# Projection of a hybrid decoder trunk: another order of memory rows, norms and key turns, five low weight halves per part on VectorE, a pause for memory keys, and a pair at the head of the second part

## The chip, the cores and the metric

The kernel runs on one core of a Trainium2 chip. The metric is the device time of one execution in microseconds (us). Engines are named as the profile names them: PE is TensorE (PEld its weight loads), ACT is ScalarE, DVE is VectorE, POOL is GpSimd, and SP is the sync engine, which issues most DMAs.

## What is computed

One mixer layer with four head groups, for a prompt of 2048 rows and for a sample group of 8 x 4 rows. Cut to what matters here:

```
h = rms_norm(x, pre_g)
z = h @ w_in                       # 1024 -> 11 x 512: ca cb cg pu pg q k v sg mq mg
mk, mv = split(rms_norm(mem_prompt, mem_g) @ w_mem_kv)
y_c = conv branch(ca, cb)          # depthwise, width 31, LayerNorm, pointwise
y_p = pool branch(pu)
y_s = stick-breaking attention(q, k, v)    # the sample group reads a paged cache of 8192 tokens
y_m = softmax attention(mq, mk, mv)        # 256 memory tokens; the sample group has its own keys
mix = [y_c*silu(cg), y_p*silu(pg), y_s*silu(sg), y_m*silu(mg)]
out = x + rms_norm(mix @ w_out, post_g); y = rms_norm(out, final_g)
```

## The kernel before

The first 1491 us of the profiled span are the projection `x @ w_in`, and everything that the change touches lies in them. It runs in two parts of 1024 prompt rows; part 0 also carries the 32 sample rows. Before any product the normalised rows of x are transposed on PE, 128 rows and 512 features at a time, and split into a high half (`xhi`, copied by ACT) and a low half (`xlo`, the difference, on DVE): `split_rows`, L211. A weight block of 1024 x 128 is loaded (`load_w`, tile `wr`, two buffers), and `split_w` (L229) makes `whi` on ACT (L232) and `wlo` on POOL (L233), two buffers each. `mm3` (L236) then multiplies a tile of up to 512 columns with 24 products: whi with xhi, whi with xlo, wlo with xhi.

PE's order is the order of the Python code (`manual_schedule` for PE). For the other engines a list scheduler orders the instructions by its own estimate of when each is ready, so a later traced instruction may be queued first; `tc.issue_after(ins)` puts the instructions of a block behind `ins` on its engine. Each engine runs its queue in order.

The order of the projection is set by these pieces:

- `GROUPS` (L762): the list of groups of weight blocks. Most groups hold one block; a pair holds two, whose column tiles alternate. The pairs are (q0, q1), (mq, sg) for c = 0, 1, 2, (mq3, pg3) and (cg3, sg3). The column tiles (`COLS`) are 384, 384 and 288 wide in part 0, 512 and 512 in part 1. `z_groups` (L789) runs them and calls `fill_w` to split the next weights as soon as a block is done.
- `Tasks`: a list of generators, each advanced by one step at every half of a column tile (12 products). `x_first` (L281) and `x_stream` (L322) bring the x rows of part 0 and part 1, `mem_norm` (L379) the two blocks of memory rows, `sample_keys` (L431) turns the sample group's memory keys (8 batches; a load into tile `mkb`, eight transposes on PE, copies into `mkbT` on ACT, a store to `mkTd`), `conv_dw` (L605) runs the taps of the convolution on DVE (tile `cacc`, L617), `mem_attend` (L494) is the memory attention of one column tile of mq (tiles `ms`, `pr`, `pT`, `pL`, `my`), and `natural` writes k and v out row by row.
- A z tile can only start when its columns of x are split: `X["done", part]`. The rows of part 1 overwrite those of part 0, so `x_stream` also waits for `X["free"]`.
- The sample group's attention over the cache (`sample_setup` L841, `sample_stages` L928) runs beside it, paced by the products issued: gathers of keys (`kt`) and values (`vt`) by POOL, `turn` (L954), which transposes keys on DVE (L959) into the single tile `T` and then issues the next gather, `scores` on PE (L972, tile `sSA`), scans on DVE (L989) and `values` on PE (L1011, tile `sO`).

Tiles of tag `k4` share four buffers: the loaded rows of `x_stream` (`xtp`), the sample keys (`mkb`, `mkbT`), the split q, k and mq tiles (`hl`, `mh`), and `pT`, `pL` of the memory attention. A buffer is free for the next tile when its last reader is done; for a stored tile that is when the store has landed. PSUM tiles of tag `tp` (three banks) hold all transposes and small products; `x_first` has five buffers for its rows.

In `x_first` two norms are ahead of the transposes: row block i is split, then i + 5 is loaded and i + 2 normalised. Six half blocks are done before the first product. `mem_norm` starts when 768 columns are split; it loads and normalises both blocks in its first step, pauses for two steps and then splits half a block at each step. Behind the projection the attention over the prompt (from L1282) and the output products follow.

Of the kernel before, what the change touches and what calls it, by code (L numbers as in the profile page):

```python
# [57 lines left out]
X0 = 6  # L58
SEND = 0.97
XA = 3  # L60
KT = 2
WR = 2

# [23 lines left out]
def kernel(  # L87
# [141 lines left out]
    def split_w(raw, nm):  # L229
        lo = wp.tile([P, ND, P], F32R, tag="wlo", name=f"wlo{nm}", bufs=2)  # L230
        hi = wp.tile([P, ND, P], F32R, tag="whi", name=f"whi{nm}", bufs=2)
        act.copy(hi, raw)  # L232
        pool.tensor_tensor(out=lo, in0=raw, in1=hi.bitcast(F32), op=ALU.subtract)  # L233
        return hi, lo

    def mm3(ps, whi, wlo, xhi, xlo, c0, c1):  # L236
# [44 lines left out]
    def x_first(tile_):  # L281

        todo = [(xp[P * t : P * (t + 1), :], P, P * t, f"p0_{t}") for t in range(8)] + [(xs, NS, PART, "s")]
        xts = {}

        def load(n):
            if n < len(todo):
                xts[n] = tile_(f"xt{todo[n][3]}")
                sp.dma_start(xts[n][: todo[n][1]], todo[n][0])

        def norm(n):
            if n < len(todo):
                norm_rows(xts[n], todo[n][1], gpre)

        def split_next():
            it = next(iter(raw))
            with tc.issue_after(table[-1].ins):
                wsplit[it] = split_w(raw.pop(it), "%d%s%d" % it)

        load(0)  # L300
        gpre = big("gpre0")[:, :D]
        sp.dma_start(gpre, pre_g[0].partition_broadcast(P))
        load(1)
        next_raw()
        load(2)
        next_raw()
        load(3)
        load(4)
        norm(0)
        norm(1)  # L310
        for i, (_, rows, col, nm) in enumerate(todo):
            for hf in range(2):
                split_rows(xts[i], rows, xhi, xlo, col, hf, nm)
                if hf:
                    X["done", 0] = col + rows
                    if i < 2:
                        split_next()
                    load(i + 5)
                    norm(i + 2)
                yield  # L320

    def x_stream(part, ahead, tile_):  # L322

        todo = [(xp[PART * part + P * t : PART * part + P * (t + 1), :], P, P * t, f"p{part}_{t}") for t in range(8)]
        ready = []
        gpre = None
        loaded = []

        def norm():
            n, xt = loaded.pop(0)  # L330
            ready.append(norm_rows(xt, todo[n][1], gpre, rs1[:, n : n + 1]))

        for i, (src, rows, col, nm) in enumerate(todo):
            while len(ready) + len(loaded) < min(len(todo), i + ahead):
                n = len(ready) + len(loaded)
                xt = tile_(f"xt{todo[n][3]}")
                sp.dma_start(xt[: todo[n][1]], todo[n][0])
                if gpre is None:
                    gpre = big(f"gpre{part}")[:, :D]
                    sp.dma_start(gpre, pre_g[0].partition_broadcast(P))  # L340
                loaded.append((n, xt))
            if i == 0:
                yield
                yield
                norm()
            if loaded:
                norm()
            while X["free"] < col + rows:
                yield
            for hf in range(2):  # L350
                split_rows(ready[i], rows, xhi, xlo, col, hf, nm)
                if hf:
                    X["done", part] = col + rows
                yield
# [24 lines left out]
    def mem_norm(mp, M):  # L379
        mg_bc = mp.tile([P, D], F32, name="mg_bc", bufs=1)  # L380
        sp.dma_start(mg_bc, mem_g[0].partition_broadcast(P))
        M["hi"] = mp.tile([P, ND, NMEM], F32R, name="mhi", bufs=1)
        M["lo"] = mp.tile([P, ND, NMEM], F32R, name="mlo", bufs=1)
        rows = []
        for t in range(2):
            xt = mp.tile([P, D], F32, tag="xt", name=f"xtm{t}", bufs=XB)
            sp.dma_start(xt, mem_prompt[0, P * t : P * (t + 1), :])
            rows.append(norm_rows(xt, P, mg_bc))
        yield
        yield  # L390
        for t in range(2):
            for hf in range(2):
                split_rows(rows[t], P, M["hi"], M["lo"], P * t, hf, f"m{t}")
                yield
# [36 lines left out]
    def sample_keys():  # L431

        for b in range(NB):
            k_ = k4(f"mkb{b}", [P, 2, 512], F32)
            sp.dma_start(k_, cmk[b].rearrange("(t p) c -> p t c", p=P))
            for _ in range(4):
                yield
            kT = k4(f"mkbT{b}", [P, 4, NMEM], F32)
            for t in range(2):
                pt = tp_tile(f"smt{b}_{t}")  # L440
                for h in range(4):
                    pe.transpose(pt[:, P * h : P * (h + 1)], k_[:, t, P * h : P * (h + 1)], ident)
                act.copy(kT[:, :, P * t : P * (t + 1)], pt.rearrange("p (h n) -> p h n", h=4))
                yield
            wq.dma_start(mkTd[b], kT)
# [48 lines left out]
    def mem_attend(h, part, c0, np_, hl, gate, kv):  # L494
# [43 lines left out]
        dve.tensor_tensor(out=mo[:, :np_], in0=yps[:, :np_], in1=gate[:, c0 : c0 + np_], op=ALU.mult)  # L538
        a = PART * part + c0
        wq.dma_start(mix_rows(12 + h, a, np_), by_tile(mo[:, :np_]))  # L540

    def mem_transpose(t2, nj, pr, pT, pL, nm):
        ps = tp_tile(f"mpt{nm}_{t2}")
# [106 lines left out]
        for r0, r1, dst in rows:  # L650
            wq.dma_start(dst, o[r0:r1])

    state = {}

    def z_open(part, kind, c):

# [23 lines left out]
    def z_evac(part, kind, c, ti, c0, c1, ps, s):  # L680
# [61 lines left out]
        elif kind == "mq":  # L742
# [4 lines left out]
                                     op0=ALU.mult, op1=ALU.subtract)  # L747
            if N > np_:
                dve.tensor_copy(mqs[:, c, :], ps[:, np_:N])
            tasks.add(mem_attend(c, part, c0, np_, hl, state["g"], s["kv"]))  # L750

    def z_close(part, kind, c, s):
# [4 lines left out]
        elif kind == "pu":  # L757
# [2 lines left out]

    MAIN = ("ca", "cb", "pu", "cg", "pg", "mg")
    GROUPS = {0: [[("q", 0), ("q", 1)]] + [[(k, c)] for k in ("q", "k", "v") for c in range(2 if k == "q" else 0, 4)],  # L762
              1: [[(k, c)] for k in ("k", "v", "q") for c in range(4)]}
    for part in range(2):
        for c in range(3):
            GROUPS[part] += [[(k, c)] for k in MAIN] + [[("mq", c), ("sg", c)]]
        GROUPS[part] += ([] if part == 0 else [[("ca", 3)], [("cb", 3)]]) + [[("pu", 3)], [("mg", 3)], [("mq", 3), ("pg", 3)]]
        GROUPS[part] += ([[("ca", 3)], [("cb", 3)]] if part == 0 else []) + [[("cg", 3), ("sg", 3)]]
    SEQ_W = [(p_,) + it for p_ in range(2) for g in GROUPS[p_] for it in g]
    for i, at in ((0, 3), (1, 4), (2, 5), (3, 7), (4, 8), (5, 9), (6, 11), (7, 12)):  # L770
        SEQ_W.insert(at, (0, "mem", i))
# [69 lines left out]
    def sample_setup(sm, S):  # L841
# [35 lines left out]
        bp = tp_tile("bps")  # L877
        pe.matmul(bp[:, 0:1], lhsT=e8, rhs=bcol, start=True, stop=True)
        dve.tensor_copy(b1, bp[:, 0:1])
        dve.tensor_scalar(out=nb1, in0=b1, scalar1=-1.0, scalar2=None, op0=ALU.mult)  # L880
        S["b1"], S["nb1"] = b1, nb1

        rep = sm.tile([P, 4, 4, 32], F32, tag="vt", name="rep", bufs=VB)
# [44 lines left out]
    def sample_stages(sm, sps, S):  # L928
# [25 lines left out]
        def turn(n, ml):  # L954
            if n < N:
                T = sm.tile([P, 4, 16, 32], F32, tag="T", name=f"T{n}_{ml}", bufs=TB)
                kt = kts.pop((n, ml))
                for hh in range(2):
                    dve.transpose(T[:, 2 * hh : 2 * hh + 2].rearrange("p s j t -> p (s j t)"),  # L959
                                  kt[:, 2 * hh : 2 * hh + 2].rearrange("p s j d -> p (s j d)"))  # L960
                Ts[n, ml] = T
                load_k(n + 1, ml)

# [60 lines left out]
        load_v(0)  # L1024
        for _ in range(Y0):
            yield
        turn(0, 0)
        for n in range(N):
            yield
            scores(n, 0)  # L1030
# [1064 lines left out]
```

## Time and profile before

| | us |
|---|---|
| median of 3 runs | 2420.67 (2415.16 to 2429.53) |
| the profiled execution | 2418.47 |
| its span | 2416.7 |
| PE busy in the span | 2285.6 (95%) |
| DVE, POOL, ACT busy | 1718.3, 1306.8, 1117.5 |

How to read it: a row of a timeline gives the start, the duration, the engine, the line of the kernel, the operation, what it writes and reads with shapes, and in brackets how long the engine had stood idle before it and what ended that. A row of the waits gives the instruction that waited, what released it, the total in us, how often, and the longest. A row of the windows gives the stretch, its length, the busy us of PE, PEld, DVE, ACT and POOL with instruction counts, the granted clock of TensorE (1.00 is full), the share of the DMA engines and GB/s.

### The profile page before, as it was taken

The page shows a single profiled execution, that of the slowest core. Times are in us where ns is not written, and L with a number is a line of the kernel's source. Part 1 is how long each engine was busy: PE and PEld are TensorE (multiplying, and loading weights), DVE is VectorE, ACT ScalarE, POOL GpSimd, SP SyncE. Part 2 cuts the span into 40 slices and gives each one's busy share as a digit, 9 for nine tenths or more (in the row PEclk, how much of TensorE's full clock was granted, in tenths as well). Part 3 has the DMA queues.
Part 4 walks back from the last instruction along what each step waited for, and adds up shares of the span by engine and source line. Part 5 has one row for each costly group of instructions (what it writes and reads, how often), then busy time and mean ns, then how long its engine had stood idle before and what let it go on. Part 6 is the DMA issues. An engine that isn't in the chain of part 4 may idle for free. (4 is left out here: it accounts for less than half of the span.)

```text
span 2416.7 us, 42137 instructions
## 1 busy us (share of the span) xinstructions
PE 2285.6 (95%) x15962; PEld 1774.5 (73%) x15962; DVE 1718.3 (71%) x2410; ACT 1117.5 (46%) x1939; POOL 1306.8 (54%) x1333
## 2 busy tenths in 40 slices
PE   7999999999999999999999998899999998989897
PEld 6998978898888777777777776455555556768775
DVE  5333774959757664587877777879798846687998
ACT  5322343242442322124242434788989954443554
POOL 2554544556574555655556564667877755453430
PEclk9999999999999999999999999999999999999998
DMA  5789988887778899987887767834333227887764
GB/s 179 223 260 298 348 290 287 284 272 263 263 254 292 277 344 325 323 287 262 275 270 269 262 218 179 239 79 117 89 88 79 64 64 242 266 272 254 245 234 170
DMA packets 340437, 562.14 MB, mean 233 GB/s; under 512 B 28481, under 2 KB 212929, under 8 KB 323834
## 3 DMA queue, kind: packets, MB, share of 16 engines
q1 hardware_dynamic: 284858, 290.72, 39.2%
q0 software_dynamic: 55376, 268.72, 31.3%
q8 instruction: 126, 2.06, 0.3%
q14 instruction: 77, 0.63, 0.1%
HBM read 469.28 MB, written 90.68 MB: 232 GB/s over the span
## 5 line engine op out<-in xcount | busy, mean ns | idle before, releaser
L959 DVE STREAM_TRANSPOSE T<-kt 128x1024 f32<-128x1024 f32 x256 | 308.9, 1226 | 183.4 <-PE sSA L972 177.2
L926 POOL DMA_INDIRECT vt<-in_cache_v_dram,idv x256 | 251.6, 983 | 242.1 <-PE sO L1011 181.5
L617 DVE SCALAR_TENSOR_TENSOR cacc<-U,par,cacc 128x512 f32<-128x512 f32 x480 | 360.2, 750 | 11.8
L1311 POOL TENSOR_TENSOR be<-be,E 128x512 f32<-128x512 f32 (+2 forms) x320 | 303.8, 957 | 118.4 <-DVE E L1302 52.4
L1302 DVE TENSOR_TENSOR_SCAN E<-gam,cr,ZM 128x513 f32<-128x513 f32 x192 | 232.8, 1262 | 15.1 <-ACT gam L1287 14.2
L926 POOL DMA_INDIRECT kt<-in_cache_k_dram,idk x128 | 126.2, 986 | 201.9 <-DVE T L959 146.8
L1322 PEld LDWEIGHTS AT<-ident,be 128*128 128x128 f32 x1088 | 117.7, 142 | 127.6 <-ACT at L1328 45.4
L1287 ACT ACTIVATE gam<-S,nbias_bc 128x1024 f32<-128x1024 f32 (+1 forms) x160 | 172.6, 1079 | 50.8 <-ACT be L1289 18.9
L1915 PE MATMUL acc<-wohi,mh 128*128 128x512 f32 (+1 forms) x480 | 193.3, 403 | 0.6 <-ACT mh L1669 0.6
L1915 PE MATMUL acc<-wolo,mh 128*128 128x512 f32 (+1 forms) x480 | 189.6, 395 | 0.0
L1915 PE MATMUL acc<-wohi,ml 128*128 128x512 f32 x448 | 178.1, 398 | 11.6 <-DVE ml L1680 11.6
L1282 PE MATMUL S<-kT,Q 128*128 128x512 f32 (+1 forms) x640 | 177.9, 401 | 6.8 <-DMA Q<-qd 2.7
L1289 ACT ACTIVATE be<-S,bias_bc 128x1024 f32<-128x1024 f32 (+1 forms) x160 | 171.6, 1073 | 0.0
L1322 PE MATMUL AT<-ident,be 128*128 128x128 f32 x1088 | 158.1, 284 | 14.1 <-ACT at L1328 4.2
L1338 PE MATMUL av<-at,V 128*64 128x512 f32 (+3 forms) x640 | 153.0, 557 | 1.7 <-DVE sbo L1343 1.7
L972 PE MATMUL sSA<-T,W 128*32 128x128 f32 x4096 | 139.2, 277 | 6.4 <-DVE T L959 5.6
L972 PEld LDWEIGHTS sSA<-T,W 128*32 128x32 f32 x4096 | 104.7, 110 | 43.6 <-issue 35.3
L1680 DVE TENSOR_TENSOR ml<-mr,mh 128x512 fp32r<-128x512 f32 x108 | 98.1, 914 | 38.4 <-ACT mh L1669 38.2
L1282 PEld LDWEIGHTS S<-kT,Q 128*128 128x128 f32 x640 | 107.1, 195 | 23.0 <-ACT be L1289 3.5
L1011 PE MATMUL sO<-vt,saT 128*32 128x512 f32 x1024 | 122.4, 592 | 0.0
L1299 DVE TENSOR_TENSOR_SCAN E<-gam,ZM 128x128 f32<-128x128 f32 (+3 forms) x128 | 96.4, 802 | 30.1 <-ACT gam L1287 25.2
L1328 ACT COPY at<-AT 128x512 f32<-128x512 f32 x192 | 108.9, 655 | 14.4 <-PE AT L1322 14.4
(571 smaller groups left out, 6043.7 us busy)
## 6 DMA issues: line engine op xcount, KB each, us to landing
Q<-qd SPq DMA_DIRECT2D x64, 256.0 KB
mr<-mixd SPq DMA_DIRECT2D x32, 512.0 KB
mr<-mixd SPq DMA_DIRECT2D x48, 256.0 KB
wor<-in_w_out_dram SPq DMA_DIRECT2D x20, 512.0 KB
xtp<-in_x_prompt_dram SPq DMA_DIRECT2D x16, 512.0 KB
kT<-kd SPq DMA_DIRECT2D x64, 128.0 KB
wor<-in_w_out_dram SPq DMA_DIRECT2D x32, 256.0 KB
msd<-mr SPq DMA_DIRECT2D x32, 256.0 KB
```

What stands on the lines that cost most here:

```text
L617: dve.scalar_tensor_tensor(out=ps, in0=U[:, a + k : a + k + H], scalar=wd[:, k : k + 1], in1=ps, op0=ALU.mult, op1=ALU.add)
L926: pool.indirect_dma_start(out=dst, out_offset=None, in_=rows, in_offset=bass.IndirectOffsetOnAxis(ap=idx, axis=0))
L959: dve.transpose(T[:, 2 * hh : 2 * hh + 2].rearrange("p s j t -> p (s j t)"), kt[:, 2 * hh : 2 * hh + 2].rearrange("p s j d -> p (s j d)"))
L972: pe.matmul(sSs[n][32 * g : 32 * g + 32, P * ml : P * (ml + 1)], lhsT=W[:, jj, :], rhs=T[:, :, jj, :], start=i == 0, stop=i == 3, tile_pos ...
L1282: pe.matmul(S[:, j, :w], lhsT=Q[hh][:, x, P * (q2 + j) : P * (q2 + j + 1)], rhs=KT[hp, hh, kc][:, :w], start=x == 0, stop=x == 1)
L1287: act.activation(out=ga[:, :, 512 - w : 512], in_=S[:, :, :w], func=AF.Sigmoid, bias=nbias_bc[:, h : h + 1], scale=-1.0)
L1289: act.activation(out=be[:, :, :w], in_=S[:, :, :w], func=AF.Sigmoid, bias=bias_bc[:, h : h + 1])
L1302: dve.tensor_tensor_scan(out=E[:, j][:, ::-1], data0=ga[:, j][:, ::-1], data1=ZM[:, 0:1].to_broadcast([P, 513]), initial=carry[hh, q2][:, ...
L1311: pool.tensor_tensor(out=be[:, j, :m], in0=be[:, j, :m], in1=E[:, j, 513 - w : 513 - w + m], op=ALU.mult)
L1322: pe.transpose(ap_[:, P * qt : P * (qt + 1)], A[hp, qb, kc, hh, qt][:, P * r : P * (r + 1)], ident)
L1338: pe.matmul(av[64 * hh : 64 * hh + 64, c], lhsT=V[:, 4 * kc + r, 64 * hh : 64 * hh + 64], rhs=ats.pop((hp, qb, kc, r, hh))[:, c], start=dg ...
L1915: pe.matmul(o[:rows], lhsT=m[a][:, k, :rows], rhs=W[prod, 4 * h + k][w], start=not cont and h == k == n == 0, stop=h == 1 and k == 3 and n ...
```

## The change

Six edits, all in the projection:

1. `mem_norm` pauses for `MSTEP = 4` steps instead of two before it splits memory rows.
2. `x_first` normalises three row blocks ahead, from the third on.
3. The low half of the second weight of a pair is made on DVE instead of POOL, unless that weight is a q or a k. These are sg0, sg1, sg2, pg3 and sg3 of both parts.
4. `sample_keys` starts no new batch while a `mem_attend` is alive (`state["att"]` counts them).
5. On DVE the first key turn is put behind the last small operation of the bias in `sample_setup`, and the norms of `x_stream` are put behind the latest key turn traced.
6. Part 1 begins with the pair (k0, k1).

```diff
+MSTEP = 4
...
-        pool.tensor_tensor(out=lo, in0=raw, in1=hi.bitcast(F32), op=ALU.subtract)
+        (dve if nm in SECOND else pool).tensor_tensor(out=lo, in0=raw, in1=hi.bitcast(F32), op=ALU.subtract)
...
         norm(0)
         norm(1)
+        ahead = 2
         for i, (_, rows, col, nm) in enumerate(todo):
...
                     load(i + 5)
-                    norm(i + 2)
+                    norm(i + ahead)
+                    if i == 2:
+                        ahead = 3
+                        norm(i + ahead)
...
         def norm():
             n, xt = loaded.pop(0)
-            ready.append(norm_rows(xt, todo[n][1], gpre, rs1[:, n : n + 1]))
+            with tc.issue_after(S["turn"].ins):
+                ready.append(norm_rows(xt, todo[n][1], gpre, rs1[:, n : n + 1]))
...
-        yield
-        yield
+        for _ in range(MSTEP):
+            yield
...
         for b in range(NB):
+            while state["att"]:
+                yield
             k_ = k4(f"mkb{b}", [P, 2, 512], F32)
...
         wq.dma_start(mix_rows(12 + h, a, np_), by_tile(mo[:, :np_]))
+        state["att"] -= 1
...
+            state["att"] += 1
             tasks.add(mem_attend(c, part, c0, np_, hl, state["g"], s["kv"]))
...
-              1: [[(k, c)] for k in ("k", "v", "q") for c in range(4)]}
+              1: [[("k", 0), ("k", 1)]] + [[(k, c)] for k in ("k", "v", "q") for c in range(2 if k == "k" else 0, 4)]}
...
+    SECOND = {"%d%s%d" % ((p_,) + g[1]) for p_ in range(2) for g in GROUPS[p_] if len(g) == 2 and g[1][0] not in "qk"}
...
-        dve.tensor_scalar(out=nb1, in0=b1, scalar1=-1.0, scalar2=None, op0=ALU.mult)
+        S["last"] = dve.tensor_scalar(out=nb1, in0=b1, scalar1=-1.0, scalar2=None, op0=ALU.mult)
...
-                    dve.transpose(T[:, 2 * hh : 2 * hh + 2].rearrange("p s j t -> p (s j t)"),
-                                  kt[:, 2 * hh : 2 * hh + 2].rearrange("p s j d -> p (s j d)"))
+                    S["turn"] = dve.transpose(T[:, 2 * hh : 2 * hh + 2].rearrange("p s j t -> p (s j t)"),
+                                              kt[:, 2 * hh : 2 * hh + 2].rearrange("p s j d -> p (s j d)"))
...
-        turn(0, 0)
+        with tc.issue_after(S["last"].ins):
+            turn(0, 0)
```

2 lines of the change are left out of this document (1 added, 1 removed).

## The prediction

> **What bounds the kernel now.** I began with the head of the page and then split the span at 1491 us, where the last projection tile ends. In the split the columns are the stretch, its length, the busy us of PE, PEld, DVE, ACT and POOL, the granted clock, the DMA share and GB/s.
>
> ```profile
> span 2416.7 us, 42137 instructions
> ...
> 0.00:1491.00 1491.00, 1447.21 (x11634) 1199.39 (x11634) 980.43 (x1348) 499.24 (x937) 793.04 (x748) 0.99 0.81 273
> 1491.00:2416.70 925.70, 838.40 (x4328) 575.16 (x4328) 737.86 (x1062) 618.22 (x1003) 513.78 (x587) 0.97 0.55 168
> ```
>
> Every edit lies in the first stretch. There PE is busy 1447 of 1491 us, while DVE has 980 (66%) and POOL 793 (53%). So the projection is PE's own queue, written out by hand, and only two things can shorten it: the 44 us in which PE stands still, and the stretches in which it runs at a lower clock. The next view is PE's waits in that stretch (total, times, longest):
>
> ```profile
> PE sSA L972 <- DVE T L959: 5.6, 4, 3.2
> PE ms L509 <- DVE pL L551: 4.7, 1, 4.7
> PE xpsp L216 <- DVE xlo L219: 3.9, 2, 2.6
> PE xpsm L216 <- DVE xtm L208: 3.7, 1, 3.7
> PE z0sg L242 <- POOL wlo0sg L233: 2.3, 2, 2.0
> ...
> PE z0q L242 <- ACT xhi L218: 1.5, 1, 1.5
> ...
> PE qps L889 <- DVE b L879: 0.9, 1, 0.9
> PE ms L509 <- DVE mh0mq L746: 0.9, 1, 0.9
> ...
> PE trcs L647 <- DVE xlo L219: 0.6, 1, 0.6
> ```
>
> Each is a single event or two, and nearly each is the place of one edit. Five of the stretches at half clock lie on them (same columns as above; the clock is the third number from the right):
>
> ```profile
> 44.34:47.76 3.42, 3.42 (x13) 3.42 (x12) 3.38 (x4) 1.09 (x4) 0.68 (x1) 0.50 0.32 117
> 146.75:150.16 3.41, 3.41 (x13) 3.31 (x13) 1.04 (x7) 0.49 (x1) 0.63 (x1) 0.50 1.09 377
> 341.30:344.72 3.42, 3.33 (x10) 3.34 (x11) 3.38 (x5) 0.00 (x0) 0.03 (x1) 0.50 0.95 345
> 365.20:372.02 6.82, 5.45 (x46) 4.78 (x47) 4.88 (x9) 1.85 (x3) 1.83 (x2) 0.50 0.37 156
> 805.52:812.34 6.82, 5.88 (x25) 4.30 (x25) 4.20 (x7) 3.46 (x7) 2.37 (x9) 0.50 0.93 344
> ```
>
> Work done at 0.50 would take half as long at full clock, so I price such a stretch at half of its busy PE time: 1.7, 1.7, 1.7, 2.7 and 2.9 us. What PE gains before 1491 us moves the whole second stretch, because its first matmuls wait on the end of the projection.
>
> **The change part by part.**
>
> Order of memory rows. The split of the memory rows comes two task steps later, behind the x rows; their loads on SP and their norms stay where they are, so no queue but PE's, and ACT's and DVE's behind it, sees another order.
>
> ```profile
> 39.53 0.60 PE L216 MATMUL xpsp<-ident,xtp 128*128 128x128 f32 x4
> 43.79 0.63 PE L216 MATMUL xpsm<-ident,xtm 128*128 128x128 f32 x4 [3.66 <-DVE xtm L208]
> ...
> 40.65 1.06 ACT L195 ACTIVATE sq<-xtm 128x1024 bf16<-128x1024 f32 x1
> ...
> 42.36 1.28 DVE L208 SCALAR_TENSOR_TENSOR xtm<-xtm,rs,mg_bc 128x1024 f32<-128x1024 f32 x1
> ```
>
> PE is free at 40.13, the normalised row is there at 43.64, and the half clock follows at once. Afterwards half a z0q tile (1.7 us at full clock, by the 44.34 row) and two groups of transposes (0.6 us and less) stand in the gap, so PE comes to the memory row near 42.9 and still waits 0.8. Gain: 3.66 + 1.7 - 1.0 = 4.4 us (bounds 2.0, if the sample rows are late in their turn, and 5.4).
>
> The x norms. From the third row on a norm is queued three rows ahead. That moves a square (1.06 us like the one above) on ACT by one row; at the z0q wait on xhi (1.5 us) the same work of the next row stands in the way. I take 0; bounds -1.5 (ACT blocked by a row that hasn't landed) and +1.5. It is needed all the same: the sample rows' norm must be ready earlier now.
>
> First key turn.
>
> ```profile
> 141.37 1.25 DVE L959 STREAM_TRANSPOSE T<-kt 128x1024 f32<-128x1024 f32 x1 [5.41 <-DMA kt<-in_cache_k_dram,idk]
> ```
>
> This turn sits on DVE ahead of the copy of the bias and holds it 5.41 us for a gather; PE pays 0.9 at qps. With the turn behind the bias that goes: 0.9. I leave the half clock behind it, as the 32 narrow qps products stay (bounds 0 and 0.9 + 1.7). The turn itself isn't later, it waits for the same gather, and the next gather of keys, which it issues on POOL, comes when it came before.
>
> The turn also orders the x norms of the second part.
>
> ```profile
> 748.65 1.28 DVE L208 SCALAR_TENSOR_TENSOR xtp<-xtp,rs,gpre 128x1024 f32<-128x1024 f32 x1 [3.96 <-DMA xtp<-in_x_prompt_dram]
> 749.86 2.36 DVE L959 STREAM_TRANSPOSE T<-kt 128x1024 f32<-128x1024 f32 x2
> ...
> 752.36 0.86 PE L972 MATMUL sSA<-T,W 128*32 128x128 f32 x24 [3.20 <-DVE T L959]
> ```
>
> A norm that was put early on DVE waits for its row, the key turn stands behind it, and the scores lose 3.20. Behind the turn the norm can't do that. It will be late instead: it ends 1.28 us after a turn, with the taps of the convolution and the x rows' lows queued behind it on DVE, and the first transposes of the second part then wait about one such norm. Gain 3.2 - 1.2 = 2.0 (bounds 0 and 3.2).
>
> Lows of second weights on VectorE: ten weights (sg four times and pg once, two parts).
>
> ```profile
> 333.14 1.05 ACT L232 CAST whi0sg<-wr0sg 128x1024 fp32r<-128x1024 f32 x1 [0.91 <-PE z0mg L242]
> ...
> 338.30 0.45 DVE L710 TENSOR_TENSOR gmg<-z0mg,sg0mg 128x288 f32<-128x288 f32 x1
> ...
> 338.82 0.21 POOL L712 COPY gms<-gmg 128x32 f32<-128x32 f32 x1 [2.23 <-DVE gmg L710]
> 339.00 2.34 POOL L233 TENSOR_TENSOR wlo0sg<-wr0sg,whi0sg 128x1024 fp32r<-128x1024 f32 x1
> ...
> 341.39 0.69 PE L242 MATMUL z0sg<-xhi,wlo0sg 128*128 128x384 f32 x1 [1.96 <-POOL wlo0sg L233]
> ...
> L208 DVE SCALAR_TENSOR_TENSOR xtp<-xtp,rs,gpre 128x1024 f32<-128x1024 f32 x16 | 20.9, 1313 | 10.3 <-DMA xtp<-in_x_prompt_dram 9.9 <-DMA gpre<-in_pre_g_dram 0.3
> ```
>
> The high half is there at 334.19, but POOL is held by a copy that waits for DVE, and then takes 2.34. The same size with two inputs from SBUF costs DVE 1.31. Even right behind gmg it ends at 340.1, where PE wanted it at 339.43. Gain: 2.3 + 1.7 - 0.8 = 3.2. DVE pays 10 x 1.31 = 13.1 us, hidden as long as it idles a third of the stretch; POOL is rid of 10 x 2.34. The lower bound is a rival below; the upper is 4.0.
>
> The row 341.30 stands behind a wait of only 1.96 us. [...]
>
> Memory keys pause.
>
> ```profile
> 352.60 0.38 SPq L435 DMA_DIRECT2D mkb<-in_cache_mem_k_dram  x1
> ...
> 357.42 0.33 SPq L445 DMA_DIRECT2D mkTd<-mkbT  x1
> ...
> 365.74 0.69 DVE L551 TENSOR_TENSOR pL<-mpt,pT 128x512 fp32r<-128x512 f32 x1 [5.43 <-DMA mkTd<-mkbT]
> ...
> 366.57 0.77 PE L509 MATMUL ms<-mkT,mh0mq 128*128 128x256 f32 x2 [4.68 <-DVE pL L551]
> ```
>
> The attention's pL takes one of the four k4 buffers and gets it only when a store of turned keys has landed. The key load at 352.60 holds another. With the pause that load isn't issued while an attention lives, so pL finds its buffer, although the store of 357.42 (begun before the pause) remains. The 4.68 and 2.7 of clock go; what is left I take as 0.9, the longest wait of a later attention without keys beside it (the mh0mq row). Gain 6.5 (bounds 0, if the remaining store still holds the buffer, and 7.4). The keys that are put off, four or five of eight, take their load and store of SP's queue and their copies on ACT with them. They are turned in the long stretch of conv and pool groups, where PE's list has no wait on them, and their readers come after 1500 us.
>
> Second part begins with a pair.
>
> ```profile
> 802.80 0.27 PE L362 MATMUL nt1k<-ident,zt1k 128*128 128x128 f32 x1
> 805.64 1.97 PE L216 MATMUL xpsp<-ident,xtp 128*128 128x128 f32 x8 [2.57 <-DVE xlo L219]
> ```
>
> After one tile of k PE has nothing to do but the transposes of the x rows that are missing, each behind ACT and DVE. The pair puts a second tile of 24 products there. Of 2.57 + 0.64 (trcs) + 0.2 and 2.9 of clock, 6.3 in all, I leave 2.0 for the last row, which still needs norm, transposes, copy and subtraction in turn (1.3 + 0.7 and less). Gain 4.3 (bounds 1 and 6.3).
>
> Sum: 4.4 + 0 + 0.9 + 2.0 + 3.2 + 6.5 + 4.3 = 21.3 us. From it I take 3 us for waits that the new order on DVE will make elsewhere: ten instructions of 1.31 ahead of key turns, on which PE already waits 5.6 in four places. That leaves 18.3. The profiled execution took 2418.5 (its span and 1.8 around it), so 2400.2; against the median of 2420.7 it is 2402.
>
> **The rivals.**
>
> DVE and POOL hold each other up. The scan that usually takes 0.8 was seen once beside a low half on POOL:
>
> ```profile
> 687.34 2.39 POOL L233 TENSOR_TENSOR wlo0pg<-wr0pg,whi0pg 128x1024 fp32r<-128x1024 f32 x1
> ...
> 688.02 2.25 DVE L989 TENSOR_TENSOR_SCAN sE<-sgam,sE,zeros 128x257 f32<-128x257 f32 x1
> ```
>
> It ends with POOL's instruction. A low half on DVE may wait as long for a POOL instruction beside it, and the key turn behind it too. If each of the ten costs PE its own length once, 13.1 of 21.3 goes back: 2412, faster by less than can be told. For it: DVE's queue is in order and has the turns. Against it: the POOL instruction that blocked was itself of the kind that leaves POOL. [...]
>
> The lows get stuck behind key turns: slower.
>
> ```profile
> DVE T L959 <- PE sSA L972: 177.2, 53, 8.8
> ```
>
> DVE waits in 53 places for scores before it may turn keys. If the low half is queued behind such a pair of turns (2.36, the 749.86 row) that waits for the scores just ahead of the weight's own tile, it is ready 2.36 + 1.31 after them, about 3.2 too late, and the clock falls (1.7): 4.9 for each. All ten cost 49 against the other 18: 2451. It turns the sign from four of ten, and passes 0.5% from seven. Against it: the high half is ready some 5 us ahead, and DVE at 338 stood in taps of the convolution, not at a turn.
>
> The pause or the order doesn't take. Keys already begun keep the buffer, and norms stay early: the 6.5 and 2.0 are missing, 2421 - 10 = 2411.
>
> Nothing new waits: all gaps close, with the x norms' 1.5, all of the memory rows' and the pair's, and both clock stretches: about 30 us, 2390.
>
> **How the numbers follow.** Forecast (2395 to 2408) 0.53; holding each other up 0.22; doesn't take 0.10; nothing waits 0.07; stuck behind turns 0.08. About 0.5%, 12 us, is what a measurement of this kernel can tell from no change: faster 0.60, the same 0.32, slower 0.08. The range 2391 to 2419 leaves out the rival of 2451 and most of that of 2390.
>
> **What would show it.** Memory rows: no wait of 3 us at xpsm, full clock right behind it. Lows: wlo0sg on DVE near 1.3 us and z0sg's wait under 1 in all four. Keys: no key load on SP between 336 and 385, no pL waiting on mkTd. Pair: xpsp's waits near 800 under 2 us in sum. Turn: no xtp wait ahead of a turn, sSA's waits not above 6. PE's idle time before the projection's end should fall from 44 to about 34, and the end from 1491 to about 1473. Wrong would be: waits on wlo from DVE, sSA's waits in tens of us, or an early end that the second stretch gives back.

## The result, and the profile after

The changed kernel takes 2410.93 us (median of 11 runs, 2407.40 to 2415.59), beside 2424.52 us for the kernel before on the same chip (2415.16 to 2430.28). The ratio is 0.9952, with a 95% interval of 0.9941 to 0.9964: 0.5% faster. Measured again beside other kernels ("the changed kernel once more" below), the same pair gave 0.9964 (0.9950 to 0.9978). So it is faster, but by 13.6 and 10.0 us of the medians instead of the 18.3 forecast. 2410.93 lies in the stated range (2391 to 2419), 9 us above the forecast of 2402 and outside its own band (2395 to 2408). The prediction took 12 us as the least that can be told from no change; the intervals here reach only some 3 us to either side.

The profiled execution after took 2411.48 us. It is only 7.0 us below the profiled one of before, because that one lay 6 us under its own median. What follows compares these two, so it has about half of the medians' difference to explain. A row's line number is that of its own kernel, so the same line stands some lines further on than in the prediction. First the head of the page, then the span split where the last projection tile ends, 1486.00 now and 1490.68 before (columns as in the prediction).

```profile
span 2409.8 us, 42118 instructions
```

```profile
0.00:1486.00 1486.00, 1445.87 (x11634) 1197.70 (x11634) 992.83 (x1358) 499.28 (x935) 773.82 (x737) 0.99 0.81 274
1486.00:2409.80 923.80, 838.08 (x4328) 574.37 (x4328) 740.44 (x1063) 618.93 (x1004) 514.22 (x587) 0.97 0.54 168
```

PE stands still for 40.1 us of the first stretch (1486.00 - 1445.87), not 44 as before and not 34 as forecast. The waits of PE in that stretch (total, times, longest) show why. Behind the wait for the first x rows (10.4, before 10.2), the old ones are mostly gone, and two new ones lead:

```profile
PE xpsp L217 <- DVE xtp L209: 10.4, 4, 8.2
PE xpss L217 <- DVE xts L209: 3.6, 1, 3.6
PE pps L485 <- DMA prow<-in_pool_scale_dram: 2.9, 1, 2.9
PE sSA L983 <- DVE T L970: 2.5, 3, 1.4
PE xpsm L217 <- DVE xtm L209: 2.2, 1, 2.2
...
PE z1k L243 <- ACT xhi L219: 2.0, 1, 2.0
...
PE xpsp L217 <- DVE xlo L220: 1.4, 1, 1.4
PE my L543 <- DVE pL L560: 1.2, 1, 1.2
PE z0sg L243 <- DVE gmg L719: 1.2, 1, 1.2
```

The wait of `ms` for `pL` (4.7) and that of `z0sg` for POOL (2.0) are no longer there, and the longest of `sSA` fell from 3.2 to 1.4. The wait of `xpsm` went from 3.7 to 2.2, but `xpss`, which had none, now waits 3.6, and `pps` waits 2.9 for a load of parameters. The stretches at half clock (the third number from the right) moved in the same way. Those at 146.75, 341.30 and 365.20 are gone, the one at 805.52 has shrunk from 6.83 to 3.41 us (now at 813.50), and the one at 44.34 has grown from 3.41 to 10.24 us (now at 45.50), with another at 76.22:

```profile
45.50:55.74 10.24, 6.76 (x33) 6.27 (x33) 6.97 (x11) 4.57 (x12) 2.00 (x2) 0.50 0.21 78
76.22:79.63 3.41, 3.41 (x18) 3.41 (x18) 0.29 (x2) 0.00 (x0) 1.00 (x1) 0.50 0.99 311
813.50:816.91 3.41, 3.41 (x10) 2.35 (x8) 2.76 (x4) 0.00 (x0) 0.00 (x0) 0.50 0.22 81
```

To see where the time went, I set the starts of the same tiles on PE side by side. The first column is the start in the kernel before, the others the difference to it, in single profiled executions. "Order" and "memory rows back" are experiments that come below.

```
first instruction on PE      before    after   memory rows  order on ACT  order, and
                                               back         added         rows back
state rows (hps)              72.71    +7.57      +1.81        -6.09         -5.02
z0sg, first                  338.81    +6.87      +2.03        -2.11         -5.17
z0ca, second                 380.47    -2.97      -7.70       -13.17        -14.86
z0ca, third                  515.47    -0.47      -6.80       -12.27        -13.96
z0ca, fourth                 720.99    +0.77      -7.04       -11.72        -13.37
z0cg, fourth                 758.40    -2.94      -9.42       -14.62        -17.26
z1v, first                   867.29    -5.41     -11.07       -15.79        -19.68
end of the projection       1490.68    -4.68     -11.46       -15.56        -19.67
```

Read the column "after" from top to bottom. The opening loses 7.6 us. The low halves and the pause of the keys gain 9.8 between 339 and 380, and 2.5 of that is given back by 515. The order of the norms gains 3.7 before 758, the pair 2.5 by 867, and the rest (-0.7, +1.2, +0.7) is small. The sum is -4.7. These are differences of single executions, and the second profile of the changed kernel shows how far they can be trusted: there the opening loses 8.0, the middle gains 11.0 and gives back 0.9, the norms gain 3.7, the pair only 1.1, and the projection ends 6.6 before that of the kernel before. A figure for one place is good to some 1.6 us. Behind the projection another 2.2 us differ (926.0 us against 923.8), but that part was between 920.0 and 925.2 us long in the experiments, with no relation to the edits, so I give it to none.

**The opening.** These are rows of ACT, PE and POOL in the changed kernel, in that order.

```profile
43.23 0.59 ACT L219 CAST xhi<-xpsp 128x512 fp32r<-128x512 f32 x1 [1.94 <-PE xpsp L217]
43.71 1.05 ACT L196 ACTIVATE sq<-xts 32x1024 bf16<-32x1024 f32 x1
...
45.09 1.04 ACT L196 ACTIVATE sq<-xtm 128x1024 bf16<-128x1024 f32 x1
...
47.82 1.04 ACT L196 ACTIVATE sq<-xtm 128x1024 bf16<-128x1024 f32 x1
...
48.86 0.48 ACT L697 ACTIVATE zt0q<-z0q 128x384 f32<-128x384 f32 x1
```

```profile
46.82 0.60 PE L217 MATMUL xpss<-ident,xts 32*128 32x32 f32 x4 [3.63 <-DVE xts L209]
49.59 1.09 PE L217 MATMUL xpsm<-ident,xtm 128*128 128x128 f32 x4 [2.16 <-DVE xtm L209]
...
75.49 0.41 PE L485 MATMUL pps<-ident,prow 36*128 36x36 f32 x4 [2.94 <-DMA prow<-in_pool_scale_dram]
```

```profile
49.81 0.99 POOL L700 TENSOR_TENSOR hl0q<-zt0q,hl0q 128x384 fp32r<-128x384 f32 x1 [18.34 <-DVE rs L200]
```

The same copy on POOL, and the last parameter load on SP, in the kernel before:

```profile
44.02 1.00 POOL L691 TENSOR_TENSOR hl0q<-zt0q,hl0q 128x384 fp32r<-128x384 f32 x1 [13.07 <-DVE rs L199]
```

```profile
53.12 0.25 SPq L456 DMA_DIRECT2D prow<-in_pool_scale_dram  x1
```

SP in the changed kernel:

```profile
32.13 1.12 SPq L393 DMA_DIRECT2D xtm<-in_mem_prompt_dram  x2
...
62.62 0.56 SPq L227 DMA_DIRECT2D wr0mem<-in_w_mem_kv_dram  x1
...
68.64 0.36 SPq L464 DMA_DIRECT2D prow<-in_pool_scale_dram  x1
```

The memory rows' first square stood at 40.65 in ACT's queue before; now it stands at 45.09, behind the copy of the last x row block (43.23) and the sample rows' square, which by edit 2 now comes ahead of it. The loads did not move: SP issued them at 31.59 then and at 32.13 now. On PE the transposes of the sample and memory rows come directly behind those of the last x row block, with no product between them, and PE waits 3.63 and 2.16 with one group of transposes (0.60) in between. The copy `zt0q` (48.86, before 43.08) is queued behind the squares as well, so POOL's `hl0q` starts 5.8 us later than before (49.81 against 44.02; POOL had nothing to do for 13.07 us ahead of it even then). SP's queue also has another order: the parameters stand behind four stores of `hl0q` and two loads of weights where they stood behind two stores, so they go out until 69.0 instead of 53.4. `pps` pays 2.94 and another 3.41 us at half clock.

**The middle.** The low half, the wait behind it, the attention's `pL`, and SP's loads of memory keys:

```profile
344.04 1.22 DVE L234 TENSOR_TENSOR wlo0sg<-wr0sg,whi0sg 128x1024 fp32r<-128x1024 f32 x1
...
363.09 0.69 DVE L560 TENSOR_TENSOR pL<-mpt,pT 128x512 fp32r<-128x512 f32 x1 [1.08 <-ACT pT L559]
```

```profile
345.68 0.44 PE L243 MATMUL z0sg<-xhi,whi0sg 128*128 128x384 f32 x1 [1.15 <-DVE gmg L719]
```

```profile
334.12 0.43 SPq L443 DMA_DIRECT2D mkb<-in_cache_mem_k_dram  x1
...
387.60 0.45 SPq L443 DMA_DIRECT2D mkb<-in_cache_mem_k_dram  x1
```

The low half takes 1.22 us on DVE, 0.09 less than priced. `z0sg` now waits 1.15 for `gmg`, which is queued behind the low half on DVE; this wait lies ahead of the tile's first product, so in the table it belongs to the stretch before. No key load is issued between 334 and 387, and `pL` waits 1.08 for ACT instead of 5.43 for a store.

### The profile page after: what moved, and what is told of

It is laid out like the page before. It is cut to its first block, busy times and chain, and to the rows that moved or that the text cites. A ratio compares the mean times of both kernels' runs of the same rounds, so it can differ in the third digit from the quotient of the medians.

```text
span 2409.8 us, 42118 instructions
## 1 busy us (share of the span) xinstructions
PE 2283.9 (95%) x15962; PEld 1772.1 (74%) x15962; DVE 1733.3 (72%) x2420; ACT 1118.2 (46%) x1939; POOL 1288.0 (53%) x1323
```

## The experiments

My theory after the comparison: five of the six edits do about what was priced, and the opening costs some 7 us because ACT's queue puts the squares of sample and memory rows behind the copies of the last x rows. The rival: the loss belongs to one execution or is hidden later, and the opening is neutral or a gain in most. In each diff the minus line is the changed kernel's, unless said otherwise. Each ratio is to the kernel before on the same chip, with its 95% interval. The changed kernel's own are 0.9952 and 0.9964, and 0.001 is 2.4 us. Where the changed kernel did not run on the same chip, I give the distance to both; two such intervals together leave it uncertain by some 4 to 5 us.

**The opening undone** (memory rows after two steps, norms two ahead):

```diff
-MSTEP = 4
+MSTEP = 2
...
-                    if i == 2:
-                        ahead = 3
-                        norm(i + ahead)
```

> The changed kernel with the two edits of the opening undone: memory rows split two steps after their loads, as before, and all x norms two rows ahead. Theory A (the opening loses time: the square of the sample rows is queued on ACT behind the last copies of the x rows, and SP's parameter loads go out some 15 us later, so that hps ends 7.6 us later than before): this kernel gets these 7 us back, up to 2 of them lost again later; 4 to 7 us faster than the changed kernel, near 2405, with z0k#0 ending within 1 us of where it ends before. Theory B (the late opening is hidden by what comes later, or belongs to one execution): within 2 us of the changed kernel. Theory C (the opening edits gain the 4.4 us of the prediction in most executions): 3 to 5 us slower than the changed kernel.

2402.42 us, ratio 0.9940 (0.9921 to 0.9959). Set against the two ratios above it is 3 to 6 us faster than the changed kernel, but the intervals overlap, so the times alone don't show it. In the trace the first z0k tile starts 2.2 us later than before instead of 7.1, and `xpsm` waits its old 3.7.

**The opening alone** (the kernel before, with edits 1 and 2 added and none of the others).

> The kernel before with the two edits of the opening alone: memory rows split two steps later, x norms three rows ahead from the third on. Theory A (the opening loses): 5 to 8 us slower than the kernel before, hps ending some 7.5 us later than before, pps waiting about 3 us for prow. Theory B (hidden later): within 2 us of before. Theory C (the prediction's term): 4.4 us faster than before.

2424.27 us, ratio 1.0028 (1.0015 to 1.0041): slower than before by 6.8 us (3.6 to 9.9). `hps` starts at 81.19 (before 72.71), `xpss` waits 3.6 and `pps` 3.0. Theory A holds, and both rivals fall: the loss isn't hidden later.

**The memory rows' place alone undone** (the first line of the diff above, `MSTEP = 2`; the norms stay three ahead).

> The changed kernel with the memory rows' step undone alone (two steps behind the loads, as before); the x norms stay three rows ahead. Theory A1 (the loss is the memory rows' place): as much faster than the changed kernel as the kernel with both undone, 4 to 7 us, and xpsm waits about 3.7 as before. Theory A2 (the loss comes from the norms three ahead, which put other work ahead of the sample rows' square): within 2 us of the changed kernel, xpss or xpsm still with a wait of 2 to 4 us and pps still waiting for prow. Theory C (prediction's term): 4 us slower.

2401.36 us, ratio 0.9933 (0.9914 to 0.9953), as with both undone, and in the trace `hps` starts 1.8 us later than before instead of 7.6. So the place is what costs. PE even waits longer at one place than before:

```profile
45.66 1.09 PE L217 MATMUL xpsm<-ident,xtm 128*128 128x128 f32 x4 [5.02 <-DVE xtm L209]
```

It waits 5.02 here, with the sample rows' square ahead of the memory rows' on ACT (41.16 and 42.54), against 3.63 + 2.16 + 2.94 in the changed kernel, and the 3.5 us behind it (45.60 to 49.10) run at a mean clock of 0.54, against 13.7 us at half clock (10.24 and 3.41) in the changed kernel's opening. The wait that the edit aimed at was the cheaper one.

**The norms alone undone** (the last three lines of the first diff; the memory rows keep their later place).

> The changed kernel with the x norms two ahead again, while the memory rows keep their later place. The prediction said that the norms three ahead are needed for the memory rows' place. If so (need): the sample rows' norm is later still, xpss waits 4 us or more, and the kernel is 1 to 3 us slower than the changed kernel. Rival (no matter): within 1.5 us of it, as with both edits undone against the memory rows alone (0.994 and 0.9933 of before). Rival (harm): the third norm in advance is what stands ahead of the sample rows' square on ACT, and the kernel is 2 us faster or more.

2407.43 us, ratio 0.9954 (0.9941 to 0.9967), while the changed kernel gave 0.9964 beside it. PE's waits in the opening have this at the top:

```profile
PE xpss L217 <- DVE xts L209: 8.5, 1, 8.5
```

The prediction's "it is needed" is right for this one wait, which grows from 3.6 to 8.5, and wrong for the time: `xpsm`'s and `pps`'s waits vanish, and the sum is nearly the same (8.5 against 3.63 + 2.16 + 2.94). The squares of all three row blocks still stand behind the last copy on ACT (43.91 to 46.89).

**An order on ACT added.** The splits of the last two x row blocks are put behind the last norm of the opening, so that ACT squares the sample and memory rows first; the rest is the changed kernel.

```diff
-                split_rows(xts[i], rows, xhi, xlo, col, hf, nm)
+                if i in (6, 7):
+                    with tc.issue_after(table[-1].ins):
+                        split_rows(xts[i], rows, xhi, xlo, col, hf, nm)
+                else:
+                    split_rows(xts[i], rows, xhi, xlo, col, hf, nm)
```

> The changed kernel with one order added: the splits of the last two x row blocks are issued behind the last norm of the opening (that of the second memory rows), so that ACT does the squares of the sample and memory rows ahead of the copies of the last x rows. Theory A (ACT's order makes the sample rows late, 3.6 at xpss, and the clock falls with it): the waits at xpss and xpsm go under 1.5 us each, the 10.2 us at half clock in the opening shrink to 3.4 or none, and the kernel is 3 to 8 us faster than the changed kernel. Rival (the squares wait for rows whose loads land late, so that the copies behind them are late instead): z0q waits for xhi of rows 6 and 7 by 2 to 5 us, and the time is within 3 us of the changed kernel or slower.

2399.48 us, ratio 0.9923 (0.9904 to 0.9941). ACT's queue in this kernel, then PE's:

```profile
31.73 1.05 ACT L196 ACTIVATE sq<-xts 32x1024 bf16<-32x1024 f32 x1
...
35.76 1.06 ACT L196 ACTIVATE sq<-xtm 128x1024 bf16<-128x1024 f32 x1 [0.35 <-DMA xtm<-in_mem_prompt_dram]
...
37.17 1.06 ACT L196 ACTIVATE sq<-xtm 128x1024 bf16<-128x1024 f32 x1
...
38.78 0.58 ACT L219 CAST xhi<-xpsp 128x512 fp32r<-128x512 f32 x1
```

```profile
42.32 0.43 PE L217 MATMUL xpss<-ident,xts 32*128 32x32 f32 x4
42.68 0.66 PE L217 MATMUL xpsm<-ident,xtm 128*128 128x128 f32 x4
```

The sample rows can be squared at 31.73 and the memory rows at 35.76: they had long landed when the changed kernel squared them at 43.71 and 45.09. Both transposes start without a wait. The same stretch of the changed kernel and of this one, 36 to 80 us:

```profile
36.00:80.00 44.00, 35.27 (x218) 34.07 (x217) 19.15 (x26) 14.70 (x30) 13.01 (x11) 0.84 0.36 114
```

```profile
36.00:80.00 44.00, 42.13 (x303) 40.80 (x302) 25.02 (x41) 17.85 (x34) 21.05 (x16) 1.00 0.53 165
```

With the order PE is busy 42.13 of 44 us at full clock, without it 35.27 at 0.84. The opening ends 6.1 us before that of the kernel before, which is more than the 4.4 that the prediction had given to the edit; in this execution 4.0 of it is lost again before 339, in the next experiment nothing. The order on ACT also changes SP's queue: the last parameter load goes out at 57.06, and `pps` doesn't wait. The rival (late copies instead) fails: `z0q` waits for no `xhi` more than 1.5, as before.

**The order, and the memory rows' old place** (the diff above and `MSTEP = 2`).

> The changed kernel with both: the memory rows' earlier place (two steps) and the order on ACT that puts the squares of sample and memory rows ahead of the copies of the last two x row blocks. Theory A (ACT's order is the cause, the place matters only through it): near the kernel with the order and the later place, 0.992 of before, xpsm's wait under 1.5 us. Rival (the place itself is right once the order holds): PE reaches the memory rows before their norm is through, xpsm waits 2 us or more with a stretch at half clock, and this kernel is 2 to 4 us slower than the one with the order and four steps.

2400.67 us, ratio 0.9920 (0.9907 to 0.9933). PE is busy 42.13 of the 44 us again, and `xpsm`'s wait is down to

```profile
PE xpsm L217 <- DVE xlo L220: 0.5, 1, 0.5
```

So with the order the place makes no difference that can be told, and without it the later place costs some 5 to 7 us by the ratios. The order on ACT was what the old wait needed. On the same chip the changed kernel ran at 2407.95; by the medians this version is 7.3 us faster, and 17.2 us faster than before.

**The changed kernel once more**, for that comparison.

> The changed kernel once more, unchanged, on the chip of the three kernels beside it, so that they can be set against it directly. Expected: 0.995 of the kernel before, as in its own comparison, and the same opening (xpss waits 3.6, pps 2.9, 10 us at half clock).

2407.95 us, ratio 0.9964 (0.9950 to 0.9978). `xpss` waits 3.6, `pps` 2.9, `xpsm` 2.2, and 10.2 us run at half clock from 46 on: the opening of the changed kernel is no matter of one execution. The stretch at half clock near 150, which had gone in the first profile, is back here with 6.83 us from 151.87 on, although `qps` doesn't wait; so its absence there can't be put down to the first key turn.

**No pause of the keys.**

```diff
-            while state["att"]:
-                yield
```

> The changed kernel without the pause of the memory keys: the key loads run on while an attention lives. Theory A (the pause takes away the wait of 4.7 us at ms and two half clock stretches, and part of it comes back when the keys that were put off are turned later): 3 to 6 us slower than the changed kernel, ms waiting 4 to 5 us for pL as before and z0ca#1 ending later by 6 to 9, with 2 to 4 of these regained by the end of the projection. Theory B (all of the gain is given back when the keys are turned later): within 2 us. Theory C (prediction's full term): 6.5 us slower.

2414.41 us, ratio 0.9986 (0.9976 to 0.9996): 5 to 8 us slower than the changed kernel. DVE's and PE's rows at the first attention, and the clock there:

```profile
373.50 0.69 DVE L558 TENSOR_TENSOR pL<-mpt,pT 128x512 fp32r<-128x512 f32 x1 [7.90 <-DMA mkTd<-mkbT]
```

```profile
374.34 0.98 PE L515 MATMUL ms<-mkT,mh0mq 128*128 128x256 f32 x3 [7.14 <-DVE pL L558]
```

```profile
369.00:379.20 10.20, 4.86 (x43) 4.19 (x44) 3.71 (x8) 2.89 (x6) 2.17 (x2) 0.51 0.66 273
```

The wait for the store is back and longer than before (7.14), with 10.2 us at a clock of 0.51. Between `z0sg` and the second `z0ca` this kernel loses 8.8 us to the changed one (10.0 to its second profile). The transposes of the keys that were put off lie in the next stretch, up to the third `z0ca`: in the changed kernel the last are at 455.7, here at 439.3. That stretch takes 135.0 us here as in the kernel before, and 135.9 in every profile with the pause but one: in the first profile of the changed kernel it took 137.5. So 0.9 is given back, not the 2.5 of that profile, and the pause is worth some 8 to 9 us at its place in these traces.

**All low halves on POOL.**

```diff
-        (dve if nm in SECOND else pool).tensor_tensor(out=lo, in0=raw, in1=hi.bitcast(F32), op=ALU.subtract)
+        pool.tensor_tensor(out=lo, in0=raw, in1=hi.bitcast(F32), op=ALU.subtract)
```

> The changed kernel with all low halves on POOL, as before. Theory A (only one of the ten weights was late before, 1.96 us with a half clock stretch behind it): 2 to 4 us slower than the changed kernel, and z0sg waits about 2 us for POOL. Theory B (with the other edits the pair's weight is no longer late, or DVE pays as much at the key turns as POOL saves): within 1.5 us. Theory C (POOL's relief of 23 us is worth more than the one wait): over 5 us slower.

2411.58 us, ratio 0.9973 (0.9962 to 0.9984): 2 to 5 us slower. In the trace `z0sg` waits for POOL as before, but the clock behind it is full:

```profile
349.30 0.45 PE L243 MATMUL z0sg<-xhi,wlo0sg 128*128 128x384 f32 x1 [1.97 <-POOL wlo0sg L234]
```

```profile
349.30:352.71 3.41, 3.41 (x22) 3.41 (x23) 3.38 (x5) 0.37 (x1) 0.00 (x0) 1.00 0.96 350
```

The kernel with edits 1 and 2 alone has the same wait (2.0). Between the first product of `z0sg` and the second `z0ca` the edit is worth 1.2 us, but there the wait for `gmg` (1.15) isn't counted; from the first product of `z0mq` it is 0.1 against the changed kernel's first profile and 1.3 against its second. The projection's end differs by 0.9 and 2.8. The runs' 2 to 5 can't be told from nothing against the ratio 0.9964, whose interval overlaps.

**No pair at the head of part 1.**

```diff
-              1: [[("k", 0), ("k", 1)]] + [[(k, c)] for k in ("k", "v", "q") for c in range(2 if k == "k" else 0, 4)]}
+              1: [[(k, c)] for k in ("k", "v", "q") for c in range(4)]}
```

> The changed kernel with the second part's pair undone: it begins with one tile of k, then one of k, and so on. Theory A (the pair closes the waits near 800 us for the transposes of x rows, and halves the stretch at half clock): 2 to 4 us slower than the changed kernel; xpsp waits 2.5 us or more and 6.8 us at half clock there. Theory C (prediction's term): 4.3 us slower. Theory B (the pair only moves the wait to the first k tile): within 1.5 us.

2409.82 us, ratio 0.9976 (0.9965 to 0.9988): 3 to 6 us slower, with an interval that overlaps that of 0.9964. The waits come back, if at other instructions than before:

```profile
802.76 1.03 PE L656 MATMUL trcs<-ident,tcs 128*32 128x128 f32 x4 [2.82 <-POOL tcs L837]
808.70 0.58 PE L243 MATMUL z1k<-xlo,whi1k 128*128 128x512 f32 x1 [2.03 <-DVE xlo L220]
```

Between the fourth `z0cg` and the first `z1v` it loses 4.2 us to the changed kernel's first profile and 2.8 to its second.

**Both orders around key turns undone** (the norms of the second part are early on DVE again, and the first turn stands ahead of the bias).

```diff
-            with tc.issue_after(S["turn"].ins):
-                ready.append(norm_rows(xt, todo[n][1], gpre, rs1[:, n : n + 1]))
+            ready.append(norm_rows(xt, todo[n][1], gpre, rs1[:, n : n + 1]))
...
-        with tc.issue_after(S["last"].ins):
-            turn(0, 0)
+        turn(0, 0)
```

> The changed kernel with both orders around the key turns undone: the first turn stands ahead of the bias again, and the second part's x norms are put early on DVE again. Theory A (both waits come back: 0.9 at qps with a half clock stretch of 3.4, and 3.2 at sSA near 750): 3 to 5 us slower than the changed kernel. Prediction's terms: 0.9 + 2.0 = 2.9 us slower. Theory B (the norm behind the turn makes the second part's rows as late as the turn was early): within 1.5 us.

2414.01 us, ratio 0.9986 (0.9972 to 1.0000): 5 to 8 us slower. DVE and PE near 750:

```profile
746.61 1.28 DVE L209 SCALAR_TENSOR_TENSOR xtp<-xtp,rs,gpre 128x1024 f32<-128x1024 f32 x1 [4.31 <-DMA xtp<-in_x_prompt_dram]
747.81 2.37 DVE L969 STREAM_TRANSPOSE T<-kt 128x1024 f32<-128x1024 f32 x2
```

```profile
750.32 1.08 PE L982 MATMUL sSA<-T,W 128*32 128x128 f32 x32 [3.60 <-DVE T L969]
```

The norm waits 4.31 for its row, the turn behind it is late, and the scores wait 3.60. From the fourth `z0ca` to the fourth `z0cg` it loses 3.5 to both profiles of the changed kernel.

**The first key turn's order alone undone** (the last three lines of that diff).

> The changed kernel with the order of the first key turn alone undone; the x norms of the second part stay behind the turns. Prediction's term: 0.9 us slower, qps waiting 0.9 for the bias. With the stretch at half clock behind it: 2.6 us slower. Rival (hidden): the conv and key tiles behind it absorb it, within 0.5 us.

2408.63 us, ratio 0.9959 (0.9946 to 0.9972), against 0.9964 for the changed kernel beside it: no difference that can be told. The trace has the wait, at two thirds of its old size:

```profile
PE qps L900 <- DVE b L890: 0.6, 1, 0.6
```

## Why the prediction was right in sign and too far in size

**The step that failed is the order of memory rows.** It was put at a gain of 4.4, and the changed opening is 7.6 us later than before; with the edits of the opening alone the kernel is 6.8 us slower. The sentence that was wrong: "their loads on SP and their norms stay where they are, so no queue but PE's, and ACT's and DVE's behind it, sees another order". The loads stayed, the norms did not. The first square of the memory rows went from 40.65 to 45.09 on ACT, because the list scheduler put one more copy of x rows and the sample rows' square ahead of it. I had drawn PE to the memory row at 42.9 and left its data at 43.64. The lower bound (2.0, "if the sample rows are late in their turn") named the right place, but without a price for the clock and without SP's queue, where the parameters were then late. That ACT's order did it is shown by the order added on ACT: with it the same place of the memory rows opens 6.1 us ahead of before. SP's queue moved with it, so its share (2.94 at `pps`) isn't shown apart. Why the scheduler chose that order, no trace shows.

**The x norms** were put at 0, and that holds for the time (0.9954 without them, 0.9964 with them, beside each other). The reason given for them holds for one wait only.

**First key turn, 0.9.** By the runs it can't be told from nothing, and the wait that comes back is 0.6. Half clock near 150 comes and goes without it, as the second profile of the changed kernel showed (6.83 us from 151.87 on; none from 146 to 160 in the first).

**The turn orders the norms: 2.0.** Its place shows 3.7 against the kernel before and 3.5 against the one without it. The 1.2 that I took off for a late norm did not come.

**Low halves: 3.2.** Its place shows 0.1 to 1.3. The instruction was priced well (1.22 against 1.31), but 1.7 of the term was the clock: the kernel before has 0.50 from 341.30 on, behind a wait of 1.96, and with all low halves on POOL a wait of 1.97 at the same product is followed by 1.00 (349.30 to 352.71). What is left is a wait of 1.97 exchanged for one of 1.15.

**The pause: 6.5.** 8.8 to 10.0 at its place and 0.9 given back when the keys that were put off are turned; the runs say 5 to 8. I had written that PE's list has no wait on these transposes; that is so, and still they take PE's time where PE has none to spare.

**The pair: 4.3.** 4.2 and 2.8 against the kernel without it, 2.5 and 1.1 against before. A wait of 2.0 for `xhi` and 3.4 us at half clock are left, as I had left 2.0.

**New waits, 3.** DVE's new order made few: `gmg` 1.2 at `z0sg`, `pL` 1.2 at `my`, and nothing else of size. In the changed kernel no product waits for a low half on DVE.

Put the measured opening into the sum, and it is 18.3 - 4.4 - 7.6 = 6.3 us, beside 4.7 and 6.6 at the projection's end of the two profiles. That it comes so near is partly luck: the low halves and the pair brought less than their terms, the pause and the order of the norms more. It is luck too that the time stayed in the range, with one term wrong by 12 us. The runs say 10.0 and 13.6; between them and the 7.0 of the profiled pair some 3 to 7 us stay open, since each profile shows one execution and the kernel before spreads over 6 to 15 us on a chip.

**The rivals.** The time is that of "hold each other up" (2412) and of "doesn't take" (2411), but neither is what happened. With the low halves on DVE the scans have not become longer:

```profile
L1000 DVE TENSOR_TENSOR_SCAN sE<-sgam,sE,zeros x62: 706/712/2132, 197.2 to 1446.2; 128x257 f32<-128x257 f32 x62
```

The longest is 2132 ns; before it was 2252, and four of them are over 1.2 us where five were (the prediction knew of one). All nine run beside a low half on POOL of 2.39 or 2.40 us and end 0.54 to 0.56 us after it (688.02 + 2.25 against 687.34 + 2.39 in the prediction's rows). Of the ten low halves on DVE nine take 1.18 to 1.28 us and one 1.60. The pause and the order took, as shown. Nothing got stuck behind key turns. The prediction's own sign of failure, an early end that the second stretch gives back, didn't show either; the end itself came 13 us later than the 1473 named.

## What to carry to other kernels

When an edit moves a step in traced order, and a scheduler orders the other engines, ask for each of these engines where the moved step's inputs will now stand in its queue: PE's order was as predicted, and ACT's made the inputs late. Before moving the step that waits, look for what stands ahead of its producer: here three squares stood behind four copies, and one order on ACT, with the memory rows back at their old place, brought 7 us on top of the change's 10. Then look at the DMA queue too: the parameters stood behind two more stores than before and went out 15.6 us later, and a transpose far away waited 2.94 for them. And before a difference at one place is called the worth of an edit, profile the same kernel twice: here the two profiles differ by up to 1.6 us in one stretch of the projection.

## What the runs showed of the hardware

TensorE ran at half clock (0.50) in stretches of 3.41, 6.83 or 10.24 us. These are the only lengths in the projection in the kernel before, in both profiles of the changed kernel, with the norms alone undone, with the first turn's order undone, and with the order and the memory rows' old place (in the last three and the second profile of the changed kernel to within 0.02 us).

How much half clock comes with a wait doesn't follow from the wait's length in these traces. With 3.66 at `xpsm` in the kernel before it was 3.41 us. Behind 5.02 at the same place (memory rows back) it was about as much: 0.54 in the mean from 45.60 to 49.10, and products 0.17 to 0.18 us apart, as at full clock, from 49.17 on. With 3.63 and 2.16 and 0.6 us of work between them it was 10.24 in both profiles of the changed kernel, and 6.83 with the first turn's order undone; with one wait of 8.5 (norms undone) it was 10.24 too. With 1.96 at the first low product of `z0sg` it was 3.41 us in the kernel before, and behind 1.97 with all low halves on POOL there was none (1.00 from 349.30 to 352.71). So the half clock that one profile shows behind a wait is one of several outcomes, and to price it as a fixed cost of that wait, as the prediction did, can be off by a stretch of 3.41 us.

The prediction took work at 0.50 to need half the time at full clock, which makes 1.7 us for such a stretch. The products come near that: in the kernel before, those of `z0q` with 384 columns start 0.32 us apart at half clock (44.17 to 47.37) and 0.17 to 0.19 apart at full clock (37.78 to 39.36). By these, 3.41 us at half clock cost some 1.5.
